# An interleaved rotary embedding: the fp32 head of batch 0 is three positions instead of four

## The chip, the core and the metric

The kernel runs on one core of one Trainium2 chip. It uses four of the core's engines: VectorE does all of the arithmetic, GpSimd, ScalarE and SyncE only issue transfers. Transfers between the chip's memory and the on-chip buffers are carried by 16 DMA engines, which take packets from several queues: GpSimd's (q0, which can convert fp32 to bf16 on the way), ScalarE's (q10) and SyncE's (q1).

The metric is the device time of one execution in microseconds. The kernel before has a median of 316.08 us over three runs (316.03 to 316.14).

## The reference

```python
batch, seq_len, num_heads, head_dim = (8, 2048, 16, 64)
# x: (8, 2048, 16, 64) fp32; cos, sin: (2048, 32) fp32
x_pairs = x.reshape(batch, seq_len, num_heads, head_dim // 2, 2)
x1 = x_pairs[..., 0]
x2 = x_pairs[..., 1]
cos = cos[None, :, None, :]
sin = sin[None, :, None, :]
out1 = x1 * cos - x2 * sin
out2 = x1 * sin + x2 * cos
out = np.stack([out1, out2], axis=-1).reshape(batch, seq_len, num_heads, head_dim)
```

Each pair of neighbouring numbers is turned by an angle that depends on the position in the sequence and the place in the head. 67 MB are read and 67 MB written.

## The kernel before, in words

**Tiling.** A batch has 2048 positions of 16 heads of 64 numbers, so 1024 numbers per position. The 128 partitions each take 16 neighbouring positions (`K` = 16), so one batch is a tile of 128 rows of 16 x 1024 numbers, and a row is 64 KB of fp32 in memory. There are eight batches. On the chip, the data is held in bf16 in one buffer of five places of a batch each (`buf`, called xt in the profile, `NX` = 5); `at` says which place a batch uses: batches 0 to 7 use places 4, 0, 1, 2, 3, 4, 0, 1. So batch 5 takes the place of batch 0, and batches 6 and 7 those of batches 1 and 2.

**Loads and stores.** `load` (L57) and `store` (L60) are issued by GpSimd, and convert between fp32 in memory and bf16 in the buffer. One call can carry one or two batches, and a range of positions.

**The arithmetic.** `rotate` works on one batch or on a range of its positions with three VectorE operations: qt = x times the sine table (L79), x = x times the cosine table in place (L85), and x plus qt with the two members of each pair swapped (L91). The tables hold the sines with alternating signs (s_tab, L104 and L105) and the cosines twice each (c_tab, L106), both bf16, made from the fp32 inputs sin_sb and cos_sb.

**The start.** The first positions of batch 0, `HEAD` of them, come in another way (L94, L95): ScalarE issues a plain fp32 transfer into the tile head (st in the profile), and VectorE casts it to bf16 into the buffer (L102). GpSimd issues, in this order, the rest of batch 0 (L57), cos (L97), sin (L98), batch 1 and batch 2. VectorE's order is: L102, the tables (L104, L105, L106), the rotation of the head's positions, the rotation of the rest of batch 0, then batch 1.

**The order.** It is written out by hand under a manual schedule: each engine issues its instructions in the order of the code, and waits where an instruction needs what another engine or a transfer has not finished. The store of batch 0 is held back on purpose by a one-element copy (L84), which VectorE does after 14 of the 16 positions of the first operation of batch 1 (`GATE`). After it GpSimd issues the load of batches 3 and 4, then that of batch 5, which waits for the store of batch 0. The last four positions of batch 7 (`TAIL`) are written in fp32 to another part of the buffer and stored by SyncE (L136); the one-element copy of L134 keeps them until the store of batch 6 has landed.

Of the kernel before, what the change touches and what calls it, by code (L numbers as in the profile page):

```python
# [2 lines left out]

# [4 lines left out]


@with_exitstack  # L10
def kernel(
    ctx: ExitStack,
    tc: tile.TileContext,
    x: bass.AP,
    cos: bass.AP,
    sin: bass.AP,
    out: bass.AP,
):
    nc = tc.nc
    fp32 = mybir.dt.float32  # L20
    bf16 = mybir.dt.bfloat16
    mult = mybir.AluOpType.mult
    add = mybir.AluOpType.add

    B, S, H, D = x.shape
    P = 128
    K = S // P
    D2 = D // 2
    HD = H * D
    NX = 5  # L30
    HEAD = 4
    TAIL = 4
    GATE = 14

    x_t = x.rearrange("b (p k) h d -> p b k (h d)", p=P, k=K)
    out_t = out.rearrange("b (p k) h d -> p b k (h d)", p=P, k=K)
    cos_t = cos.rearrange("(p k) c -> p (k c)", p=P, k=K)
    sin_t = sin.rearrange("(p k) c -> p (k c)", p=P, k=K)

    consts = ctx.enter_context(tc.tile_pool(name="consts", bufs=1))  # L40
    rows_pool = ctx.enter_context(tc.tile_pool(name="rows", bufs=1))
    stage = ctx.enter_context(tc.tile_pool(name="stage", bufs=1))

    cos_sb = consts.tile([P, K * D2], fp32)
    sin_sb = consts.tile([P, K * D2], fp32)
    c_tab = consts.tile([P, K, D], bf16)
    s_tab = consts.tile([P, K, D], bf16)


    buf = rows_pool.tile([P, NX, K, HD], bf16, name="xt")  # L50
    at = [4, 0, 1, 2, 3, 4, 0, 1]

    def place(b, n=1, k0=0, k1=K):
        return buf[:, at[b] : at[b] + n, k0:k1]

    def load(b, n=1, k0=0, k1=K):
        nc.gpsimd.dma_start(out=place(b, n, k0, k1), in_=x_t[:, b : b + n, k0:k1])  # L57

    def store(b, n=1, k0=0, k1=K):
        nc.gpsimd.dma_start(out=out_t[:, b : b + n, k0:k1], in_=place(b, n, k0, k1))  # L60

    def rotate(b, k0=0, k1=K, gate=None, to=None):
        nk = k1 - k0
        xp = buf[:, at[b], k0:k1]
        qt = stage.tile([P, K, HD], bf16, name="qt", tag="work")

        def rows(a):
            return a.rearrange("p k (h e) -> p k h e", h=H, e=D)

        def tab(a, j0=0, j1=nk):  # L70
            return dataclasses.replace(
                a,
                offset=a.offset + (k0 + j0) * D,
                ap=[a.ap[0], [D, j1 - j0], [0, H], [1, D]],
            )


        for a, z in ((0, nk),) if gate is None else ((0, GATE), (GATE, nk)):
            nc.vector.tensor_tensor(  # L79
                out=rows(qt[:, a:z]), in0=rows(xp[:, a:z]), in1=tab(s_tab, a, z), op=mult  # L80
            )
            if z < nk:
                one = buf[:1, at[gate], 0, :1]
                nc.vector.tensor_copy(out=one, in_=one)  # L84
        nc.vector.tensor_tensor(out=rows(xp), in0=rows(xp), in1=tab(c_tab), op=mult)  # L85
        q_swap = dataclasses.replace(
            qt, offset=qt.offset + 1, ap=[qt.ap[0], [2, nk * HD // 2], [-1, 2]]
        )
        x3 = xp.rearrange("p k (a j) -> p (k a) j", j=2)
        y3 = x3 if to is None else to.rearrange("p k (a j) -> p (k a) j", j=2)  # L90
        nc.vector.tensor_tensor(out=y3, in0=x3, in1=q_swap, op=add)  # L91

    with tc.manual_schedule():
        head = stage.tile([P, TAIL, HD], fp32, name="st", tag="work")  # L94
        nc.scalar.dma_start(out=head[:, :HEAD], in_=x_t[:, 0, :HEAD])  # L95
        load(0, k0=HEAD)
        nc.gpsimd.dma_start(out=cos_sb, in_=cos_t)  # L97
        nc.gpsimd.dma_start(out=sin_sb, in_=sin_t)  # L98
        load(1)
        load(2)  # L100

        nc.vector.tensor_copy(out=buf[:, at[0], :HEAD], in_=head[:, :HEAD])  # L102
        s2 = s_tab.rearrange("p k (i j) -> p (k i) j", j=2)
        nc.vector.tensor_copy(out=s2[:, :, 0], in_=sin_sb)  # L104
        nc.vector.tensor_scalar_mul(s2[:, :, 1], sin_sb, -1.0)  # L105
        nc.vector.tensor_copy(  # L106
            out=c_tab.rearrange("p k (i j) -> p (k i) j", j=2),
            in_=cos_sb.to_broadcast([P, K * D2, 2]),
        )

        rotate(0, 0, HEAD)
        rotate(0, HEAD, K)
        rotate(1, gate=0)
        store(0)
        load(3, 2)
        load(5)
        rotate(2)
        store(1, 2)
        rotate(3)
        store(3)  # L120
        load(6, 2)
        rotate(4)
        rotate(5)
        store(4, 2)
        rotate(6)
        store(6)
        rotate(7, 0, K - TAIL)
        store(7, k1=K - TAIL)

        tail = buf[:, at[3], : 2 * TAIL].rearrange("p k e -> p (k e)").bitcast(fp32)
        tail = tail.rearrange("p (k e) -> p k e", e=HD)
        nc.vector.tensor_copy(out=buf[:1, at[6], 0, :1], in_=buf[:1, at[7], K - 1, :1])  # L134
        rotate(7, K - TAIL, K, to=tail)
        nc.sync.dma_start(out=out_t[:, 7, K - TAIL :], in_=tail)  # L136


# [1 line left out]
_INS = ['x', 'cos', 'sin']  # L140
_OUTS = [((8, 2048, 16, 64), 'float32')]


# [23 lines left out]
```

## Time and profile before

| what | value |
|---|---|
| median of three runs | 316.08 us |
| profiled execution | 316.17 us |
| its span, first to last instruction | 314.4 us |
| VectorE busy | 215.4 us (69%), 37 instructions |
| GpSimd busy | 8.6 us (3%), 18 instructions |
| read / written in memory | 67.63 MB / 67.11 MB, 429 GB/s over the span |
| ScalarE's transfer of the head, issue to landing | 14.5 us (2048 KB) |
| GpSimd's first load, issue to landing | 21.2 us (3072 KB as written) |
| sin, issue to landing | 21.4 us (256 KB) |

The profile comes from one execution. The page gives the busy time of each engine, the span in 40 slices of 7.9 us with a digit for the busy tenths of each, the DMA queues with the share that their packets took of the 16 engines' span, and the chain of work that ended last, followed back from the last instruction. "L79" is line 79 of the kernel; DVE is VectorE, POOL is GpSimd. A row of a group has: line, engine, operation, what it writes and reads, how many of it; then busy time in us and the mean of one in ns; then the idle time ahead of it. Issuing a transfer is not the transfer: the time to landing is listed on its own. Transfers that convert are counted by the bytes that they write on the chip, so 200 GB/s of a load are 400 GB/s read from memory.

### The profile page before, as it was taken

How to read it: one execution, taken by the hardware profiler on the slowest of the kernel's cores; microseconds unless marked ns; L12 is line 12 of the kernel's file. 1: busy time of each engine (PE TensorE's matmuls, PEld its weight loads, DVE VectorE, ACT ScalarE, POOL GpSimd, SP SyncE). 2: the span in 40 equal slices, each digit the busy share in tenths (PEclk: the TensorE clock that was granted, in tenths of full speed). 3: DMA queues.
4: the chain of work that ended last, by engine and by line, in shares of the span. 5: the costliest groups of instructions: out<-in, count | busy, mean ns of one | idle time of the engine just before them, and what ended most of it. 6: DMA issues, size and time to landing. Idle time of an engine off the chain costs nothing.

```text
span 314.4 us, 113 instructions
## 1 busy us (share of the span) xinstructions
DVE 215.4 (69%) x37; POOL 8.6 (3%) x18
## 2 busy tenths in 40 slices
DVE  0029999999999206999999999300009999980550
POOL 3000000100000000000000000000000000000000
DMA  8999999999999999999999999999999999999996
GB/s 253 264 284 200 200 204 263 267 400 417 317 200 200 208 258 200 200 284 517 400 400 475 459 400 400 242 225 200 200 300 434 400 400 534 400 400 400 434 500 267
DMA packets 2688, 102.24 MB, mean 325 GB/s; under 512 B 256, under 2 KB 256, under 8 KB 384
## 3 DMA queue, kind: packets, MB, share of 16 engines
q0 software_dynamic: 2400, 98.04, 96.8%
q10 hardware_dynamic: 144, 2.10, 1.8%
q1 hardware_dynamic: 144, 2.10, 1.6%
HBM read 67.63 MB, written 67.11 MB: 429 GB/s over the span
## 4 chain that ended last, share of the span: by engine, by line
DVE 62%; another core or an unknown queue 17%; DMA 17%; issue 0%; POOL 0%; DVEq 0%; PEldq 0%
DVE xt L91 21%; DVE xt L85 20%; DVE qt L79 20%; DMA out_dram<-xt 10%; DMA sin_sb<-in_sin_dram 7%; POOL xt L57 0%; DVE c_tab L106 0%; POOL cos_sb L97 0%; DVE s_tab L104 0%; DVE s_tab L105 0%; DVE xt L134 0%; DVE xt L84 0%; DVEq L79 0%; PEldq L162 0%
## 5 line engine op out<-in xcount | busy, mean ns | idle before, releaser
L79 DVE TENSOR_TENSOR qt<-xt,s_tab 128x16384 bf16<-128x16384 bf16 (+4 forms) x11 | 69.9, 6360 | 53.7 <-DMA xt<-in_x_dram 53.5
L91 DVE TENSOR_TENSOR xt<-xt,qt 128x16384 bf16<-128x16384 bf16 (+3 forms) x10 | 72.0, 7198 | 0.3
L85 DVE TENSOR_TENSOR xt<-xt,c_tab 128x16384 bf16<-128x16384 bf16 (+2 forms) x10 | 69.9, 6986 | 0.3
L102 DVE CAST xt<-st 128x4096 bf16<-128x4096 f32 x1 | 2.3, 2295 | 15.2 <-DMA st<-in_x_dram 15.2
L60 POOL DMA_DIRECT2D out_dram<-xt x6 | 3.6, 604 | 221.0 <-DVE xt L91 165.3
L134 DVE COPY xt<-xt 1x1 bf16<-1x1 bf16 x1 | 0.1, 144 | 12.0 <-DMA out_dram<-xt 12.0
L57 POOL DMA_DIRECT2D xt<-in_x_dram x6 | 3.8, 635 | 53.1 <-DMA out_dram<-xt 52.3
L104 DVE CAST s_tab<-sin_sb 128x512 bf16<-128x512 f32 x1 | 0.5, 451 | 6.3 <-DMA sin_sb<-in_sin_dram 6.3
L106 DVE CAST c_tab<-cos_sb 128x1024 bf16<-128x1024 f32 x1 | 0.7, 682 | 0.0
L98 POOL DMA_DIRECT2D sin_sb<-in_sin_dram x1 | 0.6, 562 | 0.0
L97 POOL DMA_DIRECT2D cos_sb<-in_cos_dram x1 | 0.6, 554 | 0.0
L105 DVE TENSOR_SCALAR s_tab<-sin_sb 128x512 bf16<-128x512 f32 x1 | 0.4, 441 | 0.0
L84 DVE COPY xt<-xt 1x1 bf16<-1x1 bf16 x1 | 0.1, 136 | 0.0
L151 POOL MEMSET const-float32-0.0<- 128x1 f32 x1 | 0.1, 98 | 0.2 <-issue 0.2
L151 POOL MEMSET const-bfloat16-1.0<- 128x1 bf16 x1 | 0.1, 101 | 0.0
L151 POOL MEMSET const-float32-1.0<- 128x1 f32 x1 | 0.1, 98 | 0.0
L151 POOL MEMSET const-uint8-127<- 128x1 uint8 x1 | 0.1, 98 | 0.0
## 6 DMA issues: line engine op xcount, KB each, us to landing
xt<-in_x_dram POOLq DMA_DIRECT2D x2, 8192.0 KB, 58.7
xt<-in_x_dram POOLq DMA_DIRECT2D x3, 4096.0 KB, 57.4
out_dram<-xt POOLq DMA_DIRECT2D x1, 6144.0 KB, 26.2
xt<-in_x_dram POOLq DMA_DIRECT2D x1, 3072.0 KB, 21.2
st<-in_x_dram ACTq DMA_DIRECT2D x1, 2048.0 KB, 14.5
out_dram<-xt SPq DMA_DIRECT2D x1, 2048.0 KB, 10.2
cos_sb<-in_cos_dram POOLq DMA_DIRECT2D x1, 256.0 KB, 21.3
sin_sb<-in_sin_dram POOLq DMA_DIRECT2D x1, 256.0 KB, 21.4
```

The source lines that it names most:

```text
L57: nc.gpsimd.dma_start(out=place(b, n, k0, k1), in_=x_t[:, b : b + n, k0:k1])
L60: nc.gpsimd.dma_start(out=out_t[:, b : b + n, k0:k1], in_=place(b, n, k0, k1))
L79: nc.vector.tensor_tensor(out=rows(qt[:, a:z]), in0=rows(xp[:, a:z]), in1=tab(s_tab, a, z), op=mult)
L85: nc.vector.tensor_tensor(out=rows(xp), in0=rows(xp), in1=tab(c_tab), op=mult)
L91: nc.vector.tensor_tensor(out=y3, in0=x3, in1=q_swap, op=add)
L97: nc.gpsimd.dma_start(out=cos_sb, in_=cos_t)
L98: nc.gpsimd.dma_start(out=sin_sb, in_=sin_t)
L102: nc.vector.tensor_copy(out=buf[:, at[0], :HEAD], in_=head[:, :HEAD])
L104: nc.vector.tensor_copy(out=s2[:, :, 0], in_=sin_sb)
L105: nc.vector.tensor_scalar_mul(s2[:, :, 1], sin_sb, -1.0)
L106: nc.vector.tensor_copy(out=c_tab.rearrange("p k (i j) -> p (k i) j", j=2), in_=cos_sb.to_broadcast([P, K * D2, 2]),)
L151: nc = _bacc.Bacc("TRN2", target_bir_lowering=False, num_devices=1)
```

## The change

`HEAD` becomes 3, and the tile of the head is declared with `HEAD` instead of `TAIL` positions. ScalarE's transfer then has rows of 12 KB instead of 16 KB (1.5 MB instead of 2 MB), GpSimd's first load has 13 positions instead of 12 (rows of 52 KB of fp32 instead of 48 KB), and VectorE's operations on batch 0 are cut at position 3 instead of 4: 3072 and 13312 elements per partition instead of 4096 and 12288. The number of instructions and of transfers, their order and their waits stay the same.

```diff
@@ -28,7 +28,7 @@
     D2 = D // 2
     HD = H * D
     NX = 5
-    HEAD = 4
+    HEAD = 3
     TAIL = 4
     GATE = 14
 
@@ -91,7 +91,7 @@
         nc.vector.tensor_tensor(out=y3, in0=x3, in1=q_swap, op=add)
 
     with tc.manual_schedule():
-        head = stage.tile([P, TAIL, HD], fp32, name="st", tag="work")
+        head = stage.tile([P, HEAD, HD], fp32, name="st", tag="work")
         nc.scalar.dma_start(out=head[:, :HEAD], in_=x_t[:, 0, :HEAD])
         load(0, k0=HEAD)
         nc.gpsimd.dma_start(out=cos_sb, in_=cos_t)
```

## The prediction

> **What bounds the kernel now.** I read the page's engine lines and slices first, then the DMA queues, then the chain that ended last, then a table of stretches around the first loads, and last the records of single DMA packets (each has a start, a duration, a queue and a size).
>
> The page's sections 1 to 3: busy shares by engine, the 40 slices, the queues.
>
> ```profile
> DVE 215.4 (69%) x37; POOL 8.6 (3%) x18
> ...
> DVE  0029999999999206999999999300009999980550
> POOL 3000000100000000000000000000000000000000
> DMA  8999999999999999999999999999999999999996
> ...
> q0 software_dynamic: 2400, 98.04, 96.8%
> q10 hardware_dynamic: 144, 2.10, 1.8%
> q1 hardware_dynamic: 144, 2.10, 1.6%
> ```
>
> VectorE is idle for 31% of the span, and its row has holes. The DMA row has none: the 16 engines are busy in every slice, and the packets of the three queues take 96.8 + 1.8 + 1.6 = 100.2% of 16 engines' span. So the time is what the 16 DMA engines need for the bytes, plus the start before the first packet and the end after the last. An edit can pay or cost only by changing the DMA engines' work or by leaving them without packets.
>
> The chain that ended last (start, length, what):
>
> ```profile
> 2.44 21.39 DMA sin_sb<-in_sin_dram
> ...
> 51.88 7.63 DVE qt L79
> 59.50 0.05 DVE xt L84
> ...
> 104.32 15.99 another core or an unknown queue
> ...
> 198.90 37.28 another core or an unknown queue
> ...
> 262.72 31.46 DMA out_dram<-xt
> ```
>
> It starts with sin, which lands at 2.44 + 21.39 = 23.83. Sin lies on GpSimd's queue behind the first load, so its landing is set by the head, that load and the tables, all of their bytes. From there VectorE works without a break to L84 at 59.5, which releases the first store. The three long waits further on are waits for DMA; each is time in which the DMA row reads 9.
>
> The stretches of the first 62 us (start and end, length, VectorE, GpSimd, clock, DMA share, GB/s; a casting load is counted by the bytes that it writes):
>
> ```profile
> 0.00:1.70 1.70, 0.00 (x0) 0.66 (x5) 1.00 0.00 0
> 1.70:5.30 3.60, 0.00 (x0) 2.38 (x5) 1.00 1.04 364
> 5.30:7.10 1.80, 0.00 (x0) 0.00 (x0) 1.00 1.02 218
> 7.10:14.40 7.30, 0.00 (x0) 0.00 (x0) 1.00 1.01 269
> 42.20:61.50 19.30, 19.20 (x6) 1.25 (x2) 1.00 1.01 217
> ```
>
> No packet moves before 1.70. From 1.70 to 5.30 only ScalarE's head moves (364 GB/s, all fp32). At 5.30 the rate falls to 218 as counted, which is one casting packet on each engine; from 7.10 the two queues alternate. By the packet records every engine starts its first head packet between 1.75 and 2.08 (mean 1.87), sends five 16 KB packets of the head, takes its first 48 KB row of the load between 5.31 and 5.76, and from there takes one of each. The head therefore does a job beside its bytes: it keeps the DMA engines busy while GpSimd's first load, issued at 1.24, is not yet there.
>
> **The change part by part.** The sum is made against the profiled execution: 316.17 us, of which 314.4 are span and 1.77 lie around it. The median of the runs shown is 316.08, 0.09 under it.
>
> *DMA bytes.* Position 3 of batch 0 moves from the head to the load. Both read fp32 from memory, so the sum read stays at 16 positions. Each DMA engine has 8 rows of each transfer, one packet per row. Intervals from the packet records: a head row of 16 KB takes 0.611 while it runs alone and 0.620 in alternation; a load row of 48 KB takes 1.810; one of 64 KB takes 2.412. The slope of a load row is 1.810/12 = 0.151 per position, and (2.412 - 1.810)/4 = 0.1505 says the same. I price the new shapes with it: 52 KB 1.961, 12 KB 0.460 alone and 0.469 in alternation. Before: 5 x 0.611 + 3 x 0.620 + 8 x 1.810 = 19.40. After, with seven head rows ahead of the first load row: 7 x 0.460 + 0.469 + 8 x 1.961 = 19.38. The sum is -0.02, all of it on the path.
>
> "HWDGE (sync/scalar) is generally faster", says the Trainium skill (DMA: Bandwidth & Descriptors, Issuing engine by pattern), where HWDGE is the path of the head and the GpSimd load is the slower one. By that sentence the moved 512 KB would go out slower than before and the sum would be above zero; the rows just given disagree, since 48 KB of the head's kind take 3 x 0.620 = 1.86 and a 48 KB load row takes 1.81. I go by the rows.
>
> *The start.* The first head packet takes 1.24 in the mean against 0.61 later, an excess of 0.63; adding the second packet, 3.74 us pass from 1.87 to the first load row at 5.61, against 5 x 0.6025 = 3.01 at the load's pace, so the ramp costs 0.73. A packet smaller by a quarter could take at most a quarter of that, -0.18; its loss could also grow, which I bound by the spread of the engines' first load rows, 5.76 - 5.61 = +0.15. I take 0, because the excess shows in the first packets and reads as waiting time, not as bytes.
>
> *Cover for the load's arrival.* With 12 KB rows the head alone lasts, on the mean engine, until 1.87 + 0.63 + 8 x 0.460 = 6.18, and until about 6.4 on the engine with the longest first packet (1.79 start, 0.90 excess). Before, the load was there by 5.31. Margin 0.9 to 1.1, so cost 0; if the cover fails, each us costs one us of the total (first rival). The load keeps its place as GpSimd's first issue, its 128 rows, and the four issues behind it.
>
> *VectorE.* L102 casts 3072 instead of 4096 elements: from 2.295 (L102) with the slope 0.52 ns per element, about 1.76. It starts when the head lands, about 10 to 12.5 instead of 15.24, and has until sin lands at 23.83; cost 0, and no gain, as the first multiply needs sin. The two rotations of batch 0 keep three instructions each. From the rows of the groups by shape, L85:
>
> ```profile
> L85 DVE TENSOR_TENSOR xt<-xt,c_tab 128x12288 bf16<-128x12288 bf16 x2 | 13.1, 6559 | 0.1
> ...
> L85 DVE TENSOR_TENSOR xt<-xt,c_tab 128x4096 bf16<-128x4096 bf16 x2 | 4.6, 2292 | 0.1
> ```
>
> The slope is (6.559 - 2.292)/8192 = 0.521 ns. New: 2.292 - 0.533 = 1.759 and 6.559 + 0.533 = 7.092. The pair is 8.851 before and after, for L79 and L91 likewise: 0. This chain matters, because its end meets the DMA queue. By the packet records the store of batch 0, issued at 59.85, has its first packets at 61.72; the 16 engines end the load of batch 2 between 61.57 and 62.02. The earliest engine waits 0.15 for it, the last has 0.30 in hand. The chain hangs on sin, and sin and the end of that load move together, so the 0.30 stays. In the later stages no DMA or VectorE instruction is changed, and nothing there can move but as a whole.
>
> Sum: -0.02 + 0 + 0 + 0, on 316.17 gives 316.15, and on the median 316.06. I say 316.05.
>
> **The rivals.** No change is what a difference under 0.2%, 0.63 us, means here, about what a measurement of this kernel can tell.
>
> *The head runs out before the load comes (slower).* Place: the DMA engines between about 6.2 and the first load row. It speaks for it that the head is shorter and that the load of 13 positions could need longer before its first packet. Against it: the wait from issue to the first row was 5.31 - 1.24 = 4.07 at most, and even if it grew with the bytes, 4.07 x 13/12 = 4.41 puts it at 5.65. Price: arrival minus 6.4 on the last engine. It costs more than 0.63 from an arrival at 7.0, that is, a wait of 5.8; arrival at 7.4 would give 317.1.
>
> *The rows of 13 positions are cut (slower).* 13 is an odd count that the trace does not show. If a 52 KB row went as 13 packets, each engine has 8 x 12 = 96 more, at 0.010 for the shortest packet interval in the records (a semaphore's) +0.96: 317.0. It decides from 63 more packets. Against it: 48 KB rows go as one packet of 24576 bytes written, in loads, and of 49152 in stores.
>
> *VectorE is slower with odd counts (slower).* All its shapes so far are even multiples of 1024. At half the rate the three operations of 3 positions gain 3 x 1.6 = 4.8, the store comes 4.8 later, 0.30 of it is in hand: 320.6. It decides from a lengthening of 0.93. Against it: 0.521 ns per element holds from 2048 (1.203) to 16384 (8.692).
>
> *The ramp shrinks (faster, but under the bound).* Smaller first packets take the -0.18, and the head's surplus over the load's pace, 8 x 0.018 = 0.14, goes too: 315.75. A gain beyond 0.63 would need nearly the whole ramp, 0.73.
>
> **How the numbers follow.** Forecast 0.70; ramp gain 0.12, of which 0.02 beyond its bound; head runs out 0.04; rows cut 0.04; odd counts 0.02; something not named 0.04 faster and 0.04 slower. Faster by over 0.2%: 0.02 + 0.04 = 0.06. Slower: 0.04 + 0.04 + 0.02 + 0.04 = 0.14. Same: 0.70 + 0.10 = 0.80. The range goes from the ramp gain, 315.7, to the forecast with the 0.15 of a longer ramp, and the 0.30 in hand at the first store lost as much again, 316.5, rounded up to 316.6; what it leaves out is 0.20.
>
> **What would show it.** In the changed kernel's profile: the DMA row with 9 from the second slice on; ScalarE's transfer to landing in 9.5 to 12 us instead of 14.5; L102 at about 1.76; sin landing at 23.7 to 23.9; L79, L85 and L91 near 1.76 and 7.09; L84 and the first store at 59.4 to 60.0; the span at 314.2 to 314.6. Wrong would be: a stretch between 5.5 and 7.5 with DMA share well under 1, a later sin, more packets than 2400 on q0, or a hole of the DMA row near 62.

## The result and the profile after

The changed kernel takes 316.60 us in the median of 18 runs (316.48 to 316.89), the kernel before 316.07 on the same chip. The ratio is 1.0015, 95% interval 1.0008 to 1.0022: slower by 0.53 us, inside the 0.2% that I called no change, but clear of the interval, and against the sign of my sum. The profiled execution took 316.81 with a span of 315.0, against 316.17 and 314.4 before: +0.64 in each.

First the page of the changed kernel: slices, queues, two rows of the groups (busy us, mean ns | idle before) and three of the transfers (us to landing).

```profile
DMA  8999999999999999999999999999999999999996
...
q0 software_dynamic: 2400, 98.30, 97.0%
q1 hardware_dynamic: 144, 2.10, 1.6%
q10 hardware_dynamic: 144, 1.57, 1.4%
...
L102 DVE CAST xt<-st 128x3072 bf16<-128x3072 f32 x1 | 1.8, 1760 | 11.3 <-DMA st<-in_x_dram 11.3
...
L104 DVE CAST s_tab<-sin_sb 128x512 bf16<-128x512 f32 x1 | 0.5, 454 | 11.5 <-DMA sin_sb<-in_sin_dram 11.5
...
xt<-in_x_dram POOLq DMA_DIRECT2D x1, 3328.0 KB, 21.9
...
st<-in_x_dram ACTq DMA_DIRECT2D x1, 1536.0 KB, 10.5
...
sin_sb<-in_sin_dram POOLq DMA_DIRECT2D x1, 256.0 KB, 22.0
```

The DMA row is as full as before, the queues send the same number of packets, the head lands at 10.5 us after its issue, L102 takes 1.760. What differs is that GpSimd's first load, which carries 13 positions, needs 21.9 instead of 21.2, and sin 22.0 instead of 21.4. The chain that ended last (start, length):

```profile
2.44 22.01 DMA sin_sb<-in_sin_dram
...
60.13 0.05 DVE xt L84
...
199.57 37.28 another core or an unknown queue
...
263.38 31.47 DMA out_dram<-xt
```

Against the chain of before, sin is longer by 0.62 (22.01 against 21.39), L84 comes 0.63 later (60.13 against 59.50), and from there all pieces keep their length to 0.03: 37.28 in both, 31.47 against 31.46. The cast that waits for sin (L104) is late by as much already, in the kernel before and then in the changed one:

```profile
23.85 0.45 DVE L104 CAST s_tab<-sin_sb 128x512 bf16<-128x512 f32 x1 [6.31 <-DMA sin_sb<-in_sin_dram]
...
24.48 0.45 DVE L104 CAST s_tab<-sin_sb 128x512 bf16<-128x512 f32 x1 [11.45 <-DMA sin_sb<-in_sin_dram]
```

All the added time is there before 24.5 us.

Sin lands when the last of the 16 DMA engines is through. By the semaphore events in the trace, which the engines send one by one, the 16 ended sin between 23.35 and 23.83 before (mean 23.63), and between 23.52 and 24.45 after (mean 23.77). The mean engine is 0.15 later, the last one 0.62: one engine lags. It lags from the head on. These are the stretches in which the engines start their first row of the load (start and end, length, VectorE, GpSimd, clock, DMA share, GB/s), first of the kernel before:

```profile
5.30:5.80 0.50, 0.00 (x0) 0.00 (x0) 1.00 3.66 786
5.80:6.20 0.40, 0.00 (x0) 0.00 (x0) 1.00 0.00 0
```

and of the changed kernel:

```profile
5.30:5.80 0.50, 0.00 (x0) 0.00 (x0) 1.00 1.87 537
5.80:6.20 0.40, 0.00 (x0) 0.00 (x0) 1.00 3.16 696
6.20:6.50 0.30, 0.00 (x0) 0.00 (x0) 1.00 0.00 0
6.50:6.60 0.10, 0.00 (x0) 0.00 (x0) 1.00 1.24 266
```

A packet counts in the stretch in which it starts. Before, 786 GB/s x 0.50 us is 393 KB (thousand bytes), 16 packets of 24576 bytes: all engines start within half a microsecond. After, the last stretch holds 266 x 0.10 = 26.6 KB, one single packet: one engine gets to its first load row at 6.54, 0.36 behind any other. By then the last engine has sent 84 KB of the head, where before it had sent 80 KB by 5.76. The difference is 0.78, of which 0.15 is for the 4 KB more; 0.63 is lost, and 0.63 is what L104 and the end are late. The records don't name the engine, but each packet starts within 0.02 us of the end of the one before it on the same engine, so the packets can be put in line. Two head packets of this engine took 0.71 and 0.92, beside 0.46 for nearly all others of that size.

### The profile page after: what moved, and what is told of

The parts are those of the page before. It is cut to its first block, busy times and chain, and to the rows that moved or that the text cites. A ratio compares the mean times of both kernels' runs of the same rounds, so it can differ in the third digit from the quotient of the medians.

```text
span 315.0 us, 113 instructions
## 1 busy us (share of the span) xinstructions
DVE 214.9 (68%) x37; POOL 8.6 (3%) x18
## 4 chain that ended last, share of the span: by engine, by line
DVE 61%; DMA 17%; another core or an unknown queue 17%; issue 0%; POOL 0%; DVEq 0%; PEldq 0%
DVE xt L91 21%; DVE xt L85 20%; DVE qt L79 20%; DMA out_dram<-xt 10%; DMA sin_sb<-in_sin_dram 7%; POOL xt L57 0%; DVE c_tab L106 0%; POOL cos_sb L97 0%; DVE s_tab L104 0%; DVE s_tab L105 0%; DVE xt L134 0%; DVE xt L84 0%; DVEq L79 0%; PEldq L162 0%
## 5 line engine op out<-in xcount | busy, mean ns | idle before, releaser
L79 DVE TENSOR_TENSOR qt<-xt,s_tab 128x16384 bf16<-128x16384 bf16 (+6 forms) x11 | 69.9, 6360 | 53.7 <-DMA xt<-in_x_dram 53.5
L91 DVE TENSOR_TENSOR xt<-xt,qt 128x16384 bf16<-128x16384 bf16 (+4 forms) x10 | 72.0, 7198 | 0.3
L85 DVE TENSOR_TENSOR xt<-xt,c_tab 128x16384 bf16<-128x16384 bf16 (+4 forms) x10 | 69.9, 6986 | 0.3
L102 DVE CAST xt<-st 128x3072 bf16<-128x3072 f32 x1 | 1.8, 1760 | 11.3 <-DMA st<-in_x_dram 11.3
L104 DVE CAST s_tab<-sin_sb 128x512 bf16<-128x512 f32 x1 | 0.5, 454 | 11.5 <-DMA sin_sb<-in_sin_dram 11.5
L84 DVE COPY xt<-xt 1x1 bf16<-1x1 bf16 x1 | 0.1, 136 | 0.0
## 6 DMA issues: line engine op xcount, KB each, us to landing
xt<-in_x_dram POOLq DMA_DIRECT2D x1, 3328.0 KB, 21.9
st<-in_x_dram ACTq DMA_DIRECT2D x1, 1536.0 KB, 10.5
cos_sb<-in_cos_dram POOLq DMA_DIRECT2D x1, 256.0 KB, 21.9
```

Of the source, the lines that this page charges most:

```text
L79: nc.vector.tensor_tensor(out=rows(qt[:, a:z]), in0=rows(xp[:, a:z]), in1=tab(s_tab, a, z), op=mult)
```

## The experiments

Two theories stood at first. A: short rows of the head leave an engine behind while the head runs alone, and the last engine sets the end. B: it is the odd cut at position 3, with 52 KB rows of the load. A stall is here a head packet that takes over 0.05 us longer than the shortest of its size in that kernel, counted from 2.7 to 5.3 us, behind the first packets. The first four runs change the size of the head, its packets without its bytes, and the load without the head. The edits are made to the changed kernel, where nothing else is said.

**Two positions.**

```diff
-    HEAD = 3
+    HEAD = 2
```

> Edit: the head has 2 positions (8 KB rows on ScalarE's queue), the load 14. Theory A (small head rows leave one DMA engine behind while the head runs alone, and the last engine sets the end): the straggler is at least as late as with three positions, and the head also ends before the load's first rows, so sin lands at 24.5 to 25.2 and the time is 316.7 to 317.5 us. Theory B (an odd cut at position 3, 52 KB rows of the load): two positions are even again and the time is that of before, 316.1. Theory C (the load's first row is simply ready no earlier than about 5.3 and the DMA engines idle until then): the head alone ends at about 5.0, the gap of some 0.4 us gives 316.4 to 316.6 with the engines still close together.

Measured: 317.35 (ratio 1.0030, 1.0017 to 1.0044), in two groups, 316.2 to 316.4 in three runs and 317.2 to 317.9 in five. In the profile one engine is 1.0 late at sin, the other 15 end by 23.71, as early as before. Its first load row starts at 5.31 and takes 0.76 longer than its size asks; its head was through before 5. The load's first rows start at 4.50 on the fastest engine. Put in line, two engines run out of head packets: they end their last ones at 4.51 and 4.66 and start the load at 5.07 and 5.31; the other 14 go on without a pause, and only the engine of 5.31 is late at sin. So the head does run out, but on two engines, not on all; the time is in A's range, but the reason is that the head is too short for these two.

**Five positions.**

```diff
-    HEAD = 3
+    HEAD = 5
```

> Edit: the head has 5 positions (20 KB rows), the load 11. Theory A: larger head rows, no straggler; the 16 engines end sin within 0.5 us, L104 starts at 23.8 to 23.9 and the time is 316.0 to 316.1 us. Theory B (odd cut, 44 KB rows): a straggler or slower rows as with three positions, 316.4 to 316.8.

Measured: 316.39 (1.0008, 0.9999 to 1.0016). A's simple form, the smaller the worse, is wrong: 20 KB rows stall too, 19 packets, none by more than 0.30. The time lies just below B's range (316.4), so an odd cut was not out at this point.

**Four positions in two transfers.** An edit of the kernel before.

```diff
-        nc.scalar.dma_start(out=head[:, :HEAD], in_=x_t[:, 0, :HEAD])
+        for j in (0, 2):
+            nc.scalar.dma_start(out=head[:, j : j + 2], in_=x_t[:, 0, j : j + 2])
```

> Edit: the head keeps 4 positions, but ScalarE issues it as two transfers of two positions each (8 KB rows, 16 packets for each DMA engine); bytes, load and VectorE are those of before. Theory A (it is the size of the head's packets): a straggler as with three positions or worse, L104 at 24.2 to 25.0, 316.4 to 317.2 us. Theory B (it is the cut between head and load): nothing of the cut is changed, 316.1 to 316.3, of which up to 0.15 for eight more packets per engine.

Measured: 316.18 (1.0004, 0.9996 to 1.0013), sin's 16 ends between 23.28 and 23.75. Rows of 8 KB do not stall at all here, so shortness alone is not the cause.

**Three positions, the load as before.**

```diff
-        load(0, k0=HEAD)
+        load(0, k0=4)
+        load(0, k0=3, k1=4)
```

> Edit: the head has 3 positions as in the changed kernel; GpSimd loads 12 positions (48 KB rows as before) and then position 3 in a transfer of its own (4 KB rows), ahead of cos. Theory A: the head is that of the changed kernel, so is the straggler: L104 at 24.4 to 24.6, 316.5 to 316.8 us. Theory B (rows of 52 KB): the load's rows are those of before, 316.1 to 316.2.

Measured: 316.73 (1.0015, 1.0006 to 1.0024), L104 at 24.52. With the load's first rows back at 48 KB the added time is all there, so B's 52 KB rows fall; the fault lies in the head's own 12 KB rows. The next four runs ask which rows.

**Three positions in rows of 8 and 4 KB.**

```diff
-        nc.scalar.dma_start(out=head[:, :HEAD], in_=x_t[:, 0, :HEAD])
+        for j, z in ((0, 2), (2, 3)):
+            nc.scalar.dma_start(out=head[:, j:z], in_=x_t[:, 0, j:z])
```

> Edit: the changed kernel (3 positions, load of 13), but ScalarE issues the head as two transfers, of 2 positions (8 KB rows) and of 1 (4 KB rows). Theory A, in the form that the earlier runs leave (the head's rows stall when their size is no power of two, 12 or 20 KB, and the last engine sets the end): no packets of the head over their usual time between 3 and 5 us, the 16 engines end sin within 0.5 us, L104 at 23.7 to 24.0, 316.0 to 316.25 us (up to 0.1 for eight more packets per engine). Theory B (cut at 3, load rows of 52 KB): as the changed kernel, L104 at 24.4 to 24.6, 316.5 to 316.8.

Measured: 316.38 (1.0009, 0.9999 to 1.0018), L104 at 24.03. The 8 KB rows don't stall; of the 4 KB rows 17 do, by at most 0.16. About half of the added time is gone, not all of it; neither theory had the number.

**Four positions in rows of 12 and 4 KB.** An edit of the kernel before.

```diff
-        nc.scalar.dma_start(out=head[:, :HEAD], in_=x_t[:, 0, :HEAD])
+        for j, z in ((0, 3), (3, 4)):
+            nc.scalar.dma_start(out=head[:, j:z], in_=x_t[:, 0, j:z])
```

> Edit: the kernel before (4 positions, load of 12), but ScalarE issues the head as two transfers, of 3 positions (12 KB rows) and of 1 (4 KB rows). Theory A (12 KB rows of the head stall): stalls between 3 and 5 us and a straggler as in the changed kernel, L104 at 24.2 to 24.6, 316.4 to 316.8 us. Theory B (cut between head and load): the cut is that of before, 316.1 to 316.25.

Measured: 317.43 (1.0046, 1.0033 to 1.0059). The 12 KB rows stall again, 12 of them, and sin's last engine ends at 24.56, in A's range. But the time has another reason on top, which the timeline of this kernel shows (its lines are one further down, L103 is the head's cast):

```profile
23.88 2.30 DVE L103 CAST xt<-st 128x4096 bf16<-128x4096 f32 x1 [23.88 <-DMA st<-in_x_dram]
26.09 0.45 DVE L105 CAST s_tab<-sin_sb 128x512 bf16<-128x512 f32 x1
```

The second transfer's rows wait their turn behind load rows, the head lands only at 23.88, and its cast now lies between sin and the tables. The store of batch 0 is then issued at 62.09 and its first packets start at 63.20, when every engine has been through with the load since 62.84 at the latest: a real hole in the DMA work. As a test of the time this run is spoilt; as one of the stalls it stands. It keeps the tile of four positions and the cut at four, so neither the head's smaller tile nor the odd cut is needed for the stalls.

**Eight and six positions.** The second run has 6 in the same place.

```diff
-    HEAD = 3
+    HEAD = 8
```

> Edit: the head has 8 positions (32 KB rows), the load 8 (32 KB rows). Theory A (no power of two): 32 KB is one, no stalls, 316.0 to 316.15 us. Theory G (any head other than 4 changes when the two queues start to alternate, and 4 happens to fit): 316.3 to 316.6, as with 5 positions.

> Edit: the head has 6 positions (24 KB rows), the load 10 (40 KB rows). Theory A: 24 KB is no power of two, so stalls between 3 and 5 us, and between 0.1 and 0.5 us over before, 316.2 to 316.6. A variant of it, in which only odd counts of positions stall: 316.0 to 316.15. Theory G: 316.3 to 316.6.

Measured: 316.25 (1.0005, 0.9997 to 1.0014) and 316.12 (0.9999, 0.9990 to 1.0008). No stalls beyond one or two, so "no power of two" is wrong for 24 KB, and theory G is wrong for six. With eight the time lies between the two ranges and decides nothing. With six positions the table cast starts where it did before:

```profile
23.76 0.45 DVE L104 CAST s_tab<-sin_sb 128x512 bf16<-128x512 f32 x1 [2.51 <-DMA sin_sb<-in_sin_dram]
```

**GpSimd's later loads held back.** The stalls fall into the time at which GpSimd issues its loads of batches 1 and 2.

```diff
         nc.gpsimd.dma_start(out=sin_sb, in_=sin_t)
+        hold = buf[:1, at[3], 0, :1]
+        nc.gpsimd.tensor_copy(out=hold, in_=head[:1, 0, :1])
         load(1)
         load(2)
```

> Edit: the changed kernel, with GpSimd's loads of batches 1 and 2 issued only once the head has landed (a one-element GpSimd copy of the head stands ahead of them), at about 11 us instead of 2.98. Theory A1 (GpSimd's work on these two loads, issued between 2.97 and 4.1, disturbs the 12 KB rows that stall at 3.5 to 4.7): no packets of the head over their usual time after 2.7, L104 at 23.7 to 24.0, 316.0 to 316.2 us. Theory A2 (the 12 KB rows stall by themselves): stalls of 0.1 to 0.5 between 3 and 5, L104 at 24.3 to 24.6, 316.5 to 316.8.

Measured: 316.67 (1.0016, 1.0007 to 1.0025), 14 stalls, the longest 0.35, with the loads issued at 12.77. A1 falls. The stalls need no other issue beside them than those of the first load and the tables.

**One engine made late.** This one tests the other half of the theory on the kernel before.

```diff
         nc.scalar.dma_start(out=head[:, :HEAD], in_=x_t[:, 0, :HEAD])
+        spare = buf[:1, at[3]].rearrange("p k e -> p (k e)").bitcast(fp32)
+        row = x_t[:1, 0].rearrange("p k e -> p (k e)")
+        nc.scalar.dma_start(out=spare[:, :8191], in_=row[:, :8191])
         load(0, k0=HEAD)
```

> Edit: the kernel before, and behind the head ScalarE issues one more transfer, a single row of 32 KB to a place that is not in use yet (8191 numbers, a prime, so that it can't be shared out and goes to one DMA engine). It adds 0.03% to the bytes, and about 1.2 us to one of 16 engines. If the last of the 16 engines sets the end: 0.75 to 1.2 us over before (1.2 less the 0.45 that this engine may be ahead), 316.85 to 317.3, the other engines' ends unchanged. If the engines share the work: 1.2/16 = 0.08, 316.1 to 316.2.

Measured: 317.67 (1.0044, 1.0032 to 1.0057), +1.53 for one row of 32 KB in 134 MB. Its transfer, and the cast that waits for sin:

```profile
xt<-in_x_dram ACTq DMA_DIRECT2D x1, 32.0 KB
```

```profile
24.94 0.45 DVE L107 CAST s_tab<-sin_sb 128x512 bf16<-128x512 f32 x1 [7.33 <-DMA sin_sb<-in_sin_dram]
```

The cast is 1.09 later than before (24.94 - 23.85), but the whole time, +1.53, lies above the expected 0.75 to 1.2. The other 15 engines end sin by 23.84, as before, and at the very end by 313.66, while the late one ends at 315.08. Of the rest, 0.42 is one packet of the same engine, its last of the load of batch 2, that took 2.86 instead of 2.43 (see the last section). That the last engine sets the end is shown; the size was not forecast.

**A head of three and a half positions.**

```diff
-        head = stage.tile([P, HEAD, HD], fp32, name="st", tag="work")
-        nc.scalar.dma_start(out=head[:, :HEAD], in_=x_t[:, 0, :HEAD])
-        load(0, k0=HEAD)
+        n = 7 * HD // 2
+        head = stage.tile([P, n], fp32, name="st", tag="work")
+        x0 = x_t[:, 0].rearrange("p k e -> p (k e)")
+        b0 = buf[:, at[0]].rearrange("p k e -> p (k e)")
+        nc.scalar.dma_start(out=head, in_=x0[:, :n])
+        nc.gpsimd.dma_start(out=b0[:, n:], in_=x0[:, n:])
...
-        nc.vector.tensor_copy(out=buf[:, at[0], :HEAD], in_=head[:, :HEAD])
+        nc.vector.tensor_copy(out=b0[:, :n], in_=head)
```

> Edit: the changed kernel with a head of three and a half positions (14 KB rows), and the load of the other twelve and a half (50 KB rows). If only rows of an odd number of 4 KB stall: none after 2.7, 316.0 to 316.2 us. If every row that is no multiple of 8 KB stalls: stalls and a straggler, 316.4 to 316.8.

Measured: 316.29 (1.0006, 0.9997 to 1.0014), six packets over by at most 0.21, L104 at 24.02. Between the two; it decides little.

**The gate taken away.**

```diff
-        rotate(1, gate=0)
         store(0)
+        rotate(1)
```

> Edit: the changed kernel without the gate: the store of batch 0 is issued when its rotation is done, at about 52.5, and L84 is gone. If the added time is the straggler's: the same as the changed kernel, 316.5 to 316.7. If it is the store that comes too late for the DMA engines, with the chain of VectorE behind sin: the added time is gone, 316.0 to 316.2.

Measured: 317.81 (1.0054, 1.0041 to 1.0066), 1.2 slower than the changed kernel, which neither theory expected. L104 is at 24.25, so the start is that of a 12 KB head. The loss comes at the other place, where load turns into store. Stretches of the changed kernel:

```profile
59.30:60.20 0.90, 0.90 (x3) 0.00 (x0) 1.00 2.53 546
60.20:61.70 1.50, 1.47 (x2) 1.22 (x2) 1.00 0.10 22
61.70:62.30 0.60, 0.60 (x1) 0.03 (x1) 1.00 3.58 1529
```

and of this one:

```profile
59.30:60.20 0.90, 0.90 (x1) 0.00 (x0) 1.00 3.76 583
60.20:61.70 1.50, 1.47 (x2) 0.00 (x0) 1.00 0.00 0
61.70:62.30 0.60, 0.60 (x1) 0.00 (x0) 1.00 0.00 0
62.30:63.00 0.70, 0.70 (x1) 0.00 (x0) 1.00 2.63 1124
```

The last load packets start at the same time, but the store's packets only after 62.30 instead of 61.70. In the records all 16 last packets of the load take 0.73 to 1.09 longer than the 2.43 of the others, with the store issued at 52.54 and, behind it, the load of batches 3 and 4 issued at 53.07 (in the changed kernel 60.48 and 61.01) waiting behind them. So the store of the changed kernel does not come too late; a much earlier one costs more.

**Seven positions, an odd start, another queue.** Three more runs for what a row must be like to stall; the second is an edit of the kernel before.

```diff
-    HEAD = 3
+    HEAD = 7
```

> Edit: the head has 7 positions (28 KB rows), the load 9 (36 KB rows). If rows of an odd number of 4 KB stall: at least 6 head packets more than 0.05 over their usual time between 2.7 and 5.3 us (8 KB to 32 KB even rows: 0 to 5), and 316.25 to 316.6 us. If only 12 and 20 KB rows do, because they are short: at most 5 such packets, 316.05 to 316.25.

```diff
-        nc.scalar.dma_start(out=head[:, :HEAD], in_=x_t[:, 0, :HEAD])
-        load(0, k0=HEAD)
+        nc.scalar.dma_start(out=head[:, :HEAD], in_=x_t[:, 0, 1 : 1 + HEAD])
+        load(0, k0=1 + HEAD)
+        load(0, k1=1)
...
-        nc.vector.tensor_copy(out=buf[:, at[0], :HEAD], in_=head[:, :HEAD])
+        nc.vector.tensor_copy(out=buf[:, at[0], 1 : 1 + HEAD], in_=head[:, :HEAD])
```

> Edit: the kernel before, with positions 1 to 4 as the head (16 KB rows that start 4 KB into the 64 KB row in memory); GpSimd loads positions 5 to 15 and then position 0 (4 KB rows), eight more packets for each DMA engine. If the start or end of a row at an odd 4 KB stalls it: more than 5 stalls between 2.7 and 5.3 us, 316.4 to 316.8 us. If it is the length alone: at most 5, 316.1 to 316.25.

```diff
-        nc.scalar.dma_start(out=head[:, :HEAD], in_=x_t[:, 0, :HEAD])
+        nc.sync.dma_start(out=head[:, :HEAD], in_=x_t[:, 0, :HEAD])
```

> Edit: the changed kernel, with the head issued by SyncE in place of ScalarE. If the stalls belong to ScalarE's queue: gone, 316.0 to 316.2 us. If to the 12 KB rows: 7 or more stalls, 316.5 to 316.8.

Measured: 316.28 (1.0005, 0.9996 to 1.0014), 316.37 (1.0008, 0.9999 to 1.0017) and 316.64 (1.0018, 1.0009 to 1.0026). Seven positions have 4 stalls of at most 0.15, so "odd" is not borne out for 28 KB by the stalls, though the time is 0.17 over. The 16 KB rows from position 1 have 2, so a row's start in memory is not what makes them stall; the time lies between the two expected ranges. From SyncE the 12 KB rows stall as from ScalarE (12, the longest 0.38): it is not the queue.

All of it in one table. Stalls are counted as said above; "rest" is the span less the start of the first table cast.

| kernel | head rows | stalls, longest | table cast starts | rest | median |
|---|---|---|---|---|---|
| before | 16 KB | 4, 0.33 | 23.85 | 290.54 | 316.07 |
| changed | 12 KB | 10, 0.46 | 24.48 | 290.56 | 316.60 |
| load of 12 and 1 | 12 KB | 11, 0.66 | 24.52 | 290.75 | 316.73 |
| loads held back | 12 KB | 14, 0.35 | 24.13 | 290.56 | 316.67 |
| from SyncE | 12 KB | 12, 0.38 | 24.26 | 290.56 | 316.64 |
| no gate | 12 KB | 7, 0.40 | 24.25 | 291.63 | 317.81 |
| two positions | 8 KB | 4, 0.11 | 24.70 | 291.07 | 317.35 |
| four in two | 8 and 8 KB | 0 | 23.77 | 290.53 | 316.18 |
| three in two | 8 and 4 KB | 17, 0.16 (all 4 KB) | 24.03 | 290.55 | 316.38 |
| three and a half | 14 KB | 6, 0.21 | 24.02 | 290.54 | 316.29 |
| four from position 1 | 16 KB | 2, 0.08 | 23.92 | 290.53 | 316.37 |
| five | 20 KB | 19, 0.30 | 24.10 | 290.55 | 316.39 |
| six | 24 KB | 2, 0.22 | 23.76 | 290.51 | 316.12 |
| seven | 28 KB | 4, 0.15 | 23.91 | 290.55 | 316.28 |

It is not the count of stalls that sets the time, but what falls on one engine: 19 stalls of 20 KB rows cost about half of what 10 of 12 KB rows did. The kernels that stand 0.15 to 0.28 over the kernel before (five, three in two, three and a half, from position 1, seven) have intervals that reach below 1, so for these the stalls carry the reading, not the time; the kernels with 12 KB rows in one transfer are clear of it. The rest is the same to 0.05 in eleven of these 14, however the start went, and in the other three the records show packets that were slow later on. Left out are the kernels in which the cast does not start at sin's landing (four positions in rows of 12 and 4 KB, eight positions) and the one with the late row. Each profile is one execution, so the cast's start and the median do not match line by line: the profiled execution with the loads held back was the fastest of its eleven (316.47).

## Why the prediction was wrong

**The bound, and that nothing behind the start moves:** right. From the landing of sin to the end the profile after is that of before, 290.56 against 290.54.

**DMA bytes, -0.02:** the slopes were right (0.458 to 0.47 for 12 KB, 1.96 for 52 KB, as priced 0.460, 0.469 and 1.961), and so was the 13th position in the load. The sum failed in that it went by the usual packet.

**The start, 0 with -0.18 to +0.15:** this is the step that failed. I took the excess for waiting in the first packets alone, and bounded its growth by the spread of the engines in one profile. It measured +0.63 on the engine that counts: ten packets of 12 KB stalled after the first ones, and two of the longer ones fell on one engine. The mean engine lost 0.15, as much as my bound. I worked out the mean engine where the end is set by the last one, though I had the 16 starts before me; the run with one late engine shows that what one of them loses is not made up by the other 15. That the time still came out at the upper end of my range, 316.6, is luck: I had made up that end of 0.15 for the start and 0.30 for the first store, and it was the start alone that took it. Of the signs of being wrong that I had named, the later sin is the one that came.

**Cover for the load's arrival:** right for three positions, no engine waited for the load. The load's rows were ready earlier than I had on most engines: from 4.50 on, in the run with two positions. That run also shows where the rival begins: at two positions, on two engines, which got their first row at 5.07 and 5.31.

**VectorE:** right. L102 took 1.760 (1.76), the rows of three and 13 positions 1.76 and 7.09 (1.759 and 7.092).

**0.30 in hand at the first store:** wrong in size. I read the 61.72 as the time at which the store was ready. In the run with the late cast it took 63.20 - 62.09 = 1.11 from issue to first packet; by that, as an estimate, the store of before, issued at 59.85, was ready at about 60.96, 1.06 ahead of the last engine. This does not explain all: four engines still paused for 0.07 to 0.16 between load and store (the first from 61.57 to 61.72) while others went over at once, and why is open. The last engine went over without a pause, in both kernels, so it changed nothing.

**Rivals:** none of the three slower ones happened, and not the faster one, whose terms give 315.73 and not 315.75 (316.05 - 0.18 - 0.14). The sentence that I weighed, "HWDGE (sync/scalar) is generally faster" (the Trainium skill, DMA: Bandwidth & Descriptors, Issuing engine by pattern), gives the sign that came, but the runs do not bear it out as the cause: the load's 52 KB rows ran at their price, and with 24 KB on ScalarE's queue the time was that of 16 KB.

**What stays open:** the stalls of each kernel are seen in one execution, and nothing here shows why rows of 12 and 20 KB stall on some engines, and rows of 8, 16 and 24 KB hardly or not. Being short, no power of two, the start in memory, the queue, and GpSimd's loads of batches 1 and 2 are out as sole causes; an odd number of 4 KB fits 4, 12 and 20 KB, and not the stalls of 28 KB.

## What to carry to other kernels

Where the DMA engines are the bound and every transfer is split evenly over all 16, price the last engine, not the mean: look at the spread of the 16 semaphore events of one early transfer, since that spread is carried to the end. A transfer that starts a kernel should have its row sizes tried on the chip, not only its bytes; here 16 and 24 KB were equal and 12 KB cost 0.53 us, all of it in the first 7 us.

## What was not expected of the hardware

Head rows of some sizes are held up for up to 0.66 us one by one, on an engine here and there, while the neighbours run at full rate (the table).

With a store, and a load behind it, queued long before the load at work ends, that load's last packet took longer on every engine: 0.73 to 1.09 us, and 1.2 us of the time, in the run without the gate. So the copy of L84, which seems only to hold the store back, is worth 1.2 us in the changed kernel. What slows these packets is not shown: which of the two queued transfers does it was not tried. In the run with the one late row a last load packet took 0.42 longer while the other engines went over to the store, but in the changed kernel the late engine was at its last load packet (60.31 to 62.74) when the others went over from 61.76 on, and that packet took the usual 2.43.
